# Sixty-four unused bytes between the on-chip pools of a two-layer decoder trunk

## The chip, the cores and the metric

The kernel runs on one core of one Trainium2 chip. The metric is device microseconds of one execution, the median of several runs.

## The reference

Two identical layers work on 512 tokens of width 1024 in float32. Each layer normalizes x, multiplies it by one combined input projection, runs four causal token mixers on parts of the result (forgetting attention, gated linear attention, retention, a state-space scan), gates and mixes them, projects back and adds to x. Then comes a SwiGLU block with 2816 hidden columns:

```python
for l in range(DEPTH):
    h = rms_norm(x, ln1[l])
    x = x + mixer_block(h, ...)        # u = h @ w_in; four mixers; gates; merged @ w_out
    h = rms_norm(x, ln2[l])
    x = x + swiglu(h, w_ffn_in[l], w_ffn_out[l])
```

Nearly all of the arithmetic is in the products with w_in, w_up_*, w_out, w_ffn_in and w_ffn_out.

## The kernel before

Activations are kept transposed: 128 channels on the partitions, 512 tokens along the free dimension, 4 bytes each. Every large product is made from matmuls of a stationary 128 x 128 block of weights and a moving block of 512 (or 256) columns. To keep float32 accuracy each operand is split in a high and a low part (`split`, L196: ScalarE copies to the rounded type, L197; VectorE subtracts, L198), and each product is three matmuls (`mm3`, L185, which calls `mm`, L183): high by high, high by low, low by high. Each matmul has a weight load of its own (128 columns), so matmuls and weight loads come in equal numbers, and the load for one matmul runs beside the matmul before it.

Weights stream in: SyncE's queue brings slabs of eight blocks (128 x 1024) to tiles `wr`, `convert` (L242) splits them to `wh` and `wl`. All three are in pool `wp`. The moving operands are:

- `xh`, `xl` (pool `bp`): the normalized x. They move in all products with w_in (512 columns) and in part of the products with w_ffn_in (256 columns).
- `t` (pool `tp`): results of the mixers and the merged sum. They move in the products with w_up_* and w_out (512 columns).
- `f` (pool `fp`): hidden activations. They move in the products with w_ffn_out (512 columns).
- `t1`, `t2`, `t3`, each with parts h and l (pool `tq`): sums of blocks of x. `strassen` (L1230) computes w_ffn_in by seven products (L1306) of 256 columns instead of eight; products 5, 6, 7 move t1, t2, t3, products 1 to 4 move quarters of xh and xl. In products 3, 5, 6, 7 the low part of the weights is a tile `l` from a pool of its own, `lp`; in products 1, 2, 4 it is `wl` from `wp`. The high part is always `wh`.

In two places the roles are turned: `wide` (L271) and `tokmajor` (L494) load xh and xl as the stationary operand, and the weights move (284 and 256 columns).

The pools are opened one behind the other and lie so in each partition. `cp`, `wp`, `bp`, `np`, `sp` live throughout; `phase` (L152) opens the pools of a mixer stage (gp, vp, bd, tp) or, at L1194, of a feed-forward stage (tq, ep, rp, lp, fp), which take each other's place. Sizes are multiples of 128 bytes except those of `cp` and `sp`. Where the tiles of a pool start, modulo 128 bytes, follows from the sizes of those before it:

| pool | holds | start modulo 128 |
|---|---|---|
| cp | x, constants | 0 (most) |
| wp | wr, wh, wl | 64 |
| bp, np | xh, xl; norm's sums | 64 |
| gp, vp, bd, tp | mixers: gates, v, states, t | 0 |
| tq, ep, rp, fp | t1 to t3; e; rq; f | 0 |
| lp | l | 0 |

Within a tile the operands of these matmuls begin at multiples of 512 bytes, so each has the remainder of its pool (the slices of `wide`, 1136 bytes apart, are the exception). The order of the instructions on each engine is set when the program is built, by the tile framework's scheduler; mixers and projections are interleaved by costs written in the code (`pull`, `drain`).

Of the kernel before, what the change touches and what calls it, by code (L numbers as in the profile page):

```python
# [10 lines left out]
F32 = mybir.dt.float32  # L11
# [7 lines left out]
P = 128  # L19
# [112 lines left out]
def trunk(ctx: ExitStack, tc: tile.TileContext, keys, qkeys, xin, pos, wst, wsq, par, ext, cst, out):  # L132
    nc = tc.nc
    V, A, G, T = nc.vector, nc.scalar, nc.gpsimd, nc.tensor

    cp = ctx.enter_context(tc.tile_pool(name="cp", bufs=1))
    wp = ctx.enter_context(tc.tile_pool(name="wp", bufs=3))
    bp = ctx.enter_context(tc.tile_pool(name="bp", bufs=1))
    np_ = ctx.enter_context(tc.tile_pool(name="np", bufs=4))
    sp = ctx.enter_context(tc.tile_pool(name="sp", bufs=3))  # L140
# [5 lines left out]
    def nm(s):  # L146
        uid[0] += 1
        return f"{s}{uid[0]}"

    pools = {}  # L150

    def phase(**bufs):  # L152
        st = ExitStack()
        for n, b in bufs.items():
            pools[n] = st.enter_context(tc.tile_pool(name=nm(n), bufs=b, reuse_waits="tile"))
        return st

    def mixers():
        return phase(gp=2, vp=2, bd=1, tp=33)
# [121 lines left out]
    scope = mixers()  # L281
# [139 lines left out]
    def layer(l, n1, scope):  # L421
# [769 lines left out]
        scope.close()  # L1191


        scope = phase(tq=1, ep=8, rp=5, lp=2, fp=9)  # L1194

        last = l == DEPTH - 1
        tb_ = {n: tuple(pools["tq"].tile([P, HK, H], F32R, tag=n + h, name=nm(n + h)) for h in "hl") for n in ("t1", "t2", "t3")}
# [232 lines left out]
    for l in range(DEPTH):  # L1430
        n1 = layer(l, n1, scope if l == 0 else mixers())
# [71 lines left out]
```

## Time and profile before

| | |
|---|---|
| median of 3 runs | 1750.88 us (1750.79 to 1751.33) |
| profiled execution | 1751.48 us, its span 1749.8 us |
| TensorE busy in the span | 1736.9 us (99%) |
| VectorE, ScalarE, GpSimd | 1215.5 (69%), 862.0 (49%), 225.9 us (13%) |
| HBM read | 191.27 MB, 111 GB/s over the span |

A matmul's duration in the trace covers its whole passage through the array, and matmuls overlap; what one of them costs is the distance from its start to the start of the next. This distance is called its gap below. In the timeline, rows of one kind that follow each other are merged (x2); starts are printed to 0.01 us, so a gap is read over many rows.

### The profile page before, as it was taken

Reading aid. Unit: us, or ns where it says so; the run is one execution under the profiler, and the core shown is the slowest. Engines: PE = TensorE matmul, PEld = TensorE weight load, DVE = VectorE, ACT = ScalarE, POOL = GpSimd, SP = SyncE. Lnnn points to the kernel's source line nnn. Section 1 sums busy time; section 2 is a strip of 40 time slices with the busy share of each in tenths; the row PEclk is TensorE's granted clock in tenths of the full one; section 3 lists DMA queues with packets and bytes.
Section 4 is the critical chain, followed back from the end, with each engine's and each line's share of the span. In section 5 each row is a group of like instructions: output and inputs, shape, how many; then the busy total and the mean of one; then the engine's idle time right before and its main releaser. Section 6 shows DMA issues by size and latency. Waiting matters only on the chain.

```text
span 1749.8 us, 25123 instructions
## 1 busy us (share of the span) xinstructions
PE 1736.9 (99%) x10140; PEld 1500.2 (86%) x10140; DVE 1215.5 (69%) x1683; ACT 862.0 (49%) x1190; POOL 225.9 (13%) x227
## 2 busy tenths in 40 slices
PE   9999999999999999999999999999999999999998
PEld 7878888888888999898988788888888898999987
DVE  5868576777667666675777666767776685666666
ACT  5425533555347455463544254335544473645543
POOL 2032120022101000000010311201220010100000
PEclk9999999999999999999999999999999999999999
DMA  6322222222236566575333222322222365656652
GB/s 202 97 83 62 86 72 85 84 85 85 84 97 171 157 140 172 130 183 108 86 102 114 68 67 73 96 73 84 85 84 85 119 169 146 147 156 140 173 107 99
DMA packets 54693, 195.00 MB, mean 111 GB/s; under 512 B 6064, under 2 KB 6448, under 8 KB 54576
## 3 DMA queue, kind: packets, MB, share of 16 engines
q1 hardware_dynamic: 45072, 160.45, 29.0%
q0 software_dynamic: 8640, 31.46, 10.4%
q8 instruction: 79, 1.29, 0.3%
q10 hardware_dynamic: 864, 1.48, 0.2%
q14 instruction: 38, 0.31, 0.1%
HBM read 191.27 MB, written 2.10 MB: 111 GB/s over the span
## 4 chain that ended last, share of the span: by engine, by line
PE 96%; DVE 2%; DMA 1%; ACT 1%; issue 0%; ACTq 0%; DVEq 0%
PE mm L183 64%; PE mx L183 31%; DVE wl L198 1%; PE mx L1058 0%; DMA x<-in_x_dram 0%; DMA t<-in_ext_dram 0%; ACT wh L197 0%; DVE f L1399 0%; DVE x L1400 0%; PE mx L658 0%; DVE t L352 0%; ACT L216 0%; ACT g L221 0%; DVE t L1147 0%; PE mx L930 0%
## 5 line engine op out<-in xcount | busy, mean ns | idle before, releaser
L197 ACT CAST wh<-wr 128x1024 fp32r<-128x1024 f32 (+1 forms) x240 | 249.8, 1042 | 394.5 <-PE mm L183 247.7
L183 PE MATMUL mm<-xh,wh 128*128 128x512 f32 (+1 forms) x1184 | 431.4, 364 | 0.8 <-DVE t L1147 0.8
L183 PE MATMUL mm<-xh,wl 128*128 128x512 f32 (+1 forms) x1184 | 430.5, 364 | 0.0
L183 PE MATMUL mm<-xl,wh 128*128 128x512 f32 (+1 forms) x1184 | 429.8, 363 | 0.0
L198 DVE TENSOR_TENSOR wl<-wr,wh 128x1024 fp32r<-128x1024 f32 (+1 forms) x220 | 282.0, 1283 | 117.9 <-ACT wh L197 109.7
L183 PEld LDWEIGHTS mm<-xh,wh 128*128 128x128 f32 x1184 | 223.5, 189 | 36.3 <-DVE t L1147 1.7
L183 PEld LDWEIGHTS mm<-xh,wl 128*128 128x128 f32 x1184 | 223.7, 189 | 34.8 <-issue 1.5
L183 PEld LDWEIGHTS mm<-xl,wh 128*128 128x128 f32 x1184 | 223.6, 189 | 33.7 <-issue 1.1
L183 PE MATMUL mm<-t,wh 128*128 128x512 f32 x448 | 142.5, 397 | 0.0
L183 PE MATMUL mx<-xl,wh 128*128 128x256 f32 (+1 forms) x448 | 140.4, 313 | 0.0
L183 PE MATMUL mx<-xh,wh 128*128 128x256 f32 (+1 forms) x448 | 137.8, 314 | 2.3 <-ACT wh L197 2.3
L1264 POOL DMA_DIRECT2D wl<-in_wsq_dram x60 | 51.9, 864 | 542.1 <-ACT wl L1263 322.9
L183 PE MATMUL mx<-f,wh 128*128 128x512 f32 x352 | 110.2, 395 | 0.0
L183 PE MATMUL mm<-f,wh 128*128 128x512 f32 x352 | 108.3, 396 | 0.0
L183 PEld LDWEIGHTS mm<-t,wh 128*128 128x128 f32 x448 | 83.2, 188 | 19.1
L198 DVE TENSOR_TENSOR l<-rq,wh 128x1024 fp32r<-128x1024 f32 x60 | 73.2, 1220 | 34.6 <-ACT wh L197 19.1
L183 PEld LDWEIGHTS mx<-xh,wh 128*128 128x128 f32 x448 | 84.6, 189 | 8.9 <-ACT wh L197 3.5
L183 PE MATMUL mx<-xh,wl 128*128 128x256 f32 (+1 forms) x288 | 91.9, 330 | 0.0
L183 PEld LDWEIGHTS mx<-xl,wh 128*128 128x128 f32 x448 | 84.7, 189 | 5.3
L183 PE MATMUL mm<-t,wl 128*128 128x512 f32 x224 | 88.5, 395 | 0.0
L183 PEld LDWEIGHTS mm<-f,wh 128*128 128x128 f32 x352 | 65.7, 188 | 16.2 <-ACT wh L197 1.0
L183 PEld LDWEIGHTS mx<-f,wh 128*128 128x128 f32 x352 | 65.4, 188 | 15.5
(275 smaller groups left out, 3470.8 us busy)
## 6 DMA issues: line engine op xcount, KB each, us to landing
wr<-in_wst_dram SPq DMA_DIRECT2D x216, 512.0 KB, 3.5
rq<-in_wsq_dram SPq DMA_DIRECT2D x60, 512.0 KB, 4.6
wl<-in_wsq_dram POOLq DMA_DIRECT2D x60, 512.0 KB, 5.7
wr<-in_wsq_dram SPq DMA_DIRECT2D x20, 512.0 KB, 5.0
out_dram<-x SPq DMA_DIRECT2D x8, 256.0 KB, 2.0
x<-in_x_dram SPq DMA_DIRECT2D x3, 512.0 KB, 6.9
wr<-in_wst_dram SPq DMA_DIRECT2D x4, 256.0 KB, 5.4
x<-in_x_dram SPq DMA_DIRECT2D x2, 256.0 KB, 4.5
```

The lines of the kernel that those rows point to most:

```text
L183: T.matmul(o, lhsT=l, rhs=r, start=start, stop=stop, skip_group_check=True)
L197: A.copy(out=hi, in_=src)
L198: V.tensor_tensor(out=lo, in0=src, in1=hi.bitcast(F32), op=ALU.subtract)
L1264: G.dma_start(out=lo, in_=wsq[j], accum_op=ALU.add)
```

## The change

No instruction is added or removed, and no wait. Pools of one tile of 64 bytes that nothing reads or writes are put between the pools:

```diff
     cp = ctx.enter_context(tc.tile_pool(name="cp", bufs=1))
+    gap = [ctx.enter_context(tc.tile_pool(name="gap0", bufs=1))]
     wp = ctx.enter_context(tc.tile_pool(name="wp", bufs=3))
+    gap.append(ctx.enter_context(tc.tile_pool(name="gap1", bufs=1)))
     bp = ctx.enter_context(tc.tile_pool(name="bp", bufs=1))
...
+    def pad(pool, n):
+        pool.tile([P, n // 4], F32, tag=nm("pad"), name=nm("pad"))
...
     def phase(**bufs):
+        if not pools:
+            for g in gap:
+                pad(g, 64)
         st = ExitStack()
+        pad(st.enter_context(tc.tile_pool(name=nm("gap"), bufs=1)), 64)
...
-        scope = phase(tq=1, ep=8, rp=5, lp=2, fp=9)
+        scope = phase(tq=1, ep=8, rp=5, g0=1, lp=2, g1=1, fp=9)
+        pad(pools["g0"], 64)
+        pad(pools["g1"], 64)
```

By the sums of the sizes, `wp` moves by 64 bytes, `bp`, `np` and `sp` by 128, the pools of a mixer stage and tq, ep, rp by 192, lp by 256, fp by 320. Modulo 128:

| pool | before | after |
|---|---|---|
| wp (wr, wh, wl) | 64 | 0 |
| bp, np (xh, xl) | 64 | 64 |
| gp, vp, bd, tp (t) | 0 | 64 |
| tq (t1 to t3), ep, rp | 0 | 64 |
| lp (l) | 0 | 0 |
| fp (f) | 0 | 64 |

So after the change the weights lie at 0 and the activations at 64 in every large product.

## Rows read from the trace of the kernel before

**Rows 1.** The page, parts 1 and 2: busy time and share of the engines (PEld is TensorE's weight load); the granted TensorE clock in 40 slices, in tenths.

```profile
PE 1736.9 (99%) x10140; PEld 1500.2 (86%) x10140; DVE 1215.5 (69%) x1683; ACT 862.0 (49%) x1190; POOL 225.9 (13%) x227
...
PEclk9999999999999999999999999999999999999999
```

**Rows 2.** TensorE's waits, whole span: engine, line, what it waited for: us in total, times, longest us. The two longest.

```profile
PE mm L183 <- DVE wl L198: 2.6, 6, 0.4
PE mx L183 <- ACT wh L197: 2.3, 3, 1.1
```

**Rows 3.** Busy time of each engine by stretch of the span (us, then busy us and instructions): the input projection with mixers, the products with w_out, the feed-forward of the first layer. The last three columns are the granted clock, the share of the DMA engines and GB/s.

```profile
178.00:466.00 288.00, 287.08 (x1549) 239.93 (x1548) 202.01 (x319) 136.72 (x192) 46.70 (x48) 1.00 0.26 81
478.00:530.00 52.00, 52.00 (x224) 41.75 (x223) 33.86 (x46) 24.23 (x32) 3.45 (x2) 1.00 0.33 105
...
555.00:875.00 320.00, 318.69 (x2177) 293.26 (x2177) 214.31 (x251) 170.62 (x229) 25.73 (x29) 1.00 0.58 142
```

**Rows 4.** Timeline of TensorE (start us, us, engine, line, operation, out<-in) in w_in's projection, weights and moving operand at 64: the first and the last of 15 matmuls in a row.

```profile
43.70 0.39 PE L183 MATMUL mm<-xh,wh 128*128 128x512 f32 x1
...
46.87 0.39 PE L183 MATMUL mm<-xh,wl 128*128 128x512 f32 x1
```

**Rows 5.** The same view in w_ffn_out, weights at 64, moving operand f at 0: from the first row's start to the last row's there are 12 matmuls.

```profile
600.42 0.63 PE L183 MATMUL mx<-f,wh 128*128 128x512 f32 x2
...
603.22 1.09 PE L183 MATMUL mx<-f,wh 128*128 128x512 f32 x4
```

**Rows 6.** The same view inside `strassen`, moving xh and xl at 64, 256 columns. First a product whose weights all lie at 64 (8 rows, the first and the last shown), then 12 matmuls of a product whose third matmul has its weights in l, at 0 (the first four and the one behind the twelfth).

```profile
568.42 0.28 PE L183 MATMUL mm<-xh,wl 128*128 128x256 f32 x1
...
569.26 0.28 PE L183 MATMUL mx<-xh,wh 128*128 128x256 f32 x1
569.38 0.28 PE L183 MATMUL mx<-xl,wh 128*128 128x256 f32 x1
569.50 0.28 PE L183 MATMUL mx<-xh,l 128*128 128x256 f32 x1
569.61 0.28 PE L183 MATMUL mx<-xh,wh 128*128 128x256 f32 x1
...
570.67 0.28 PE L183 MATMUL mm<-xh,wh 128*128 128x256 f32 x1
```

**Rows 7.** The same view where 512-column matmuls are followed by 256-column ones, all operands at 64.

```profile
553.62 0.39 PE L183 MATMUL mx<-xh,wl 128*128 128x512 f32 x1
553.85 0.28 PE L183 MATMUL mm<-xh,wh 128*128 128x256 f32 x1
553.96 0.28 PE L183 MATMUL mm<-xl,wh 128*128 128x256 f32 x1
554.08 0.28 PE L183 MATMUL mm<-xh,wl 128*128 128x256 f32 x1
554.20 0.28 PE L183 MATMUL mm<-xh,wh 128*128 128x256 f32 x1
```

**Rows 8.** The same view where one matmul with its weights at 0 (the constant cr, moving operand n at 64) stands in a row of 512-column matmuls with weights and moving operand at 64.

```profile
545.67 0.39 PE L183 MATMUL mx<-xl,wh 128*128 128x512 f32 x1
545.89 0.39 PE L183 MATMUL mx<-xh,wl 128*128 128x512 f32 x1
546.12 0.40 PE L183 MATMUL mm<-n,cr 128*128 128x512 f32 x1
546.35 0.39 PE L183 MATMUL mx<-xh,wh 128*128 128x512 f32 x1
...
547.27 0.39 PE L183 MATMUL mx<-xh,wh 128*128 128x512 f32 x1
```

**Rows 9.** Groups of matmuls by tile and shape over the whole span (xcount | busy us, mean ns of one | idle before): the first and the last of the eight groups that move t or f over 512 columns (1,920 matmuls), then of the six that move xh or xl over 512 (2,976), the seven that move xh or xl over 256 (1,920), the nine that move t1 to t3 over 256 (160 each, 1,440), and one of the three in which the weights move over 256 (128 each).

```profile
L183 PE MATMUL mm<-t,wh 128*128 128x512 f32 x448 | 142.5, 397 | 0.0
...
L183 PE MATMUL mx<-t,wl 128*128 128x512 f32 x64 | 25.2, 394 | 0.0
...
L183 PE MATMUL mm<-xh,wh 128*128 128x512 f32 x864 | 340.7, 394 | 0.8 <-DVE t L1147 0.8
...
L183 PE MATMUL mx<-xh,wl 128*128 128x512 f32 x128 | 46.7, 390 | 0.0
...
L183 PE MATMUL mm<-xh,wh 128*128 128x256 f32 x320 | 90.6, 283 | 0.0
...
L183 PE MATMUL mx<-xh,l 128*128 128x256 f32 x160 | 44.5, 278 | 0.0
...
L183 PE MATMUL mm<-t3l,wh 128*128 128x256 f32 x160 | 44.8, 281 | 0.0
...
L183 PE MATMUL mm<-t2h,l 128*128 128x256 f32 x160 | 42.1, 282 | 0.0
...
L183 PE MATMUL mm<-wh,xh 128*128 128x256 f32 x128 | 36.2, 283 | 0.0
```

**Rows 10.** Groups of VectorE's instructions by tile and shape, whole span: the subtraction of `split` with all its tiles at 64, and with rq and l at 0.

```profile
L198 DVE TENSOR_TENSOR wl<-wr,wh 128x1024 fp32r<-128x1024 f32 x216 | 278.4, 1290 | 117.6 <-ACT wh L197 109.7 <-PE mm L183 5.8 <-PE mx L183 1.2
L198 DVE TENSOR_TENSOR l<-rq,wh 128x1024 fp32r<-128x1024 f32 x60 | 73.2, 1220 | 34.6 <-ACT wh L197 19.1 <-PE mm L183 15.2
```

## The prediction

> **What bounds the kernel now.** I read the page first: TensorE is busy in 99% of the span, its clock is granted in full in every slice (the 2.4 GHz level), and no other engine passes 69% [rows 1]. Its waits for others come to a few us in all [rows 2]. So nothing in front of TensorE sets the time: the 10,140 matmuls do, one gap after the other. The stretches say the same of each stage: in the feed-forward VectorE works 214 of 320 us and the DMA engines 58% [rows 3], so there is room for a faster TensorE. Then I went to the timeline for the gap itself. At 2.4 GHz, 512 columns are 213.3 ns and 256 are 106.7. Nowhere is a gap that short:
>
> - xh, xl at 64 over weights at 64, 512 columns: 14 gaps in 3.17 us, 226.4 ns each [rows 4].
> - f at 0 over weights at 64, 512 columns: 12 gaps in 2.80 us, 233.3 ns [rows 5].
> - xh, xl at 64 over weights at 64, 256 columns: 7 gaps in 0.84 us, 120 ns [rows 6].
> - the same with every third matmul's weights in l, at 0: 12 gaps in 1.41 us, 117.5 ns, and the gap that is short in each three is that of the matmul over l, 0.11 us [rows 6].
>
> The excess is 13 to 20 ns per matmul, 10,140 times; it is all that an edit without instructions can win. 233.3 and 226.7, and 120 and 113.3, are 6.67 ns apart, 16 columns or 64 bytes of moving operand. So the excess seems to come in steps of 64 bytes. That is my reading of four rows, not something that a view prints.
>
> **The change, part by part.** It adds no instruction, DMA or wait, and no queue is passed; SyncE's and GpSimd's queues keep their order. All that moves is where a tile starts.
>
> *Moving t and f over 512 columns, 1,920 matmuls [rows 9].* They go from 0 to 64, their weights from 64 to 0. Rows 4 and 5 differ in the moving operand's half alone (the same tiles of weights, line and shape): 64 is better by 233.3 - 226.4 = 6.9 ns. In w_ffn_out (22 blocks x 8 columns x 3 x 2 layers = 1,056) and w_out (8 x 8 x 3 x 2 = 384) such matmuls follow each other without a break: 1,440 x 6.9 = 9.9 us. The 480 of w_up lie between mixer matmuls, and the means over the whole span (397 against 394 ns, breaks included [rows 9]) differ by less; I take half, 480 x 3.4 = 1.6 us. Together -11.5 us. Bounds: 0, and two steps instead of one (-25.6 us).
>
> *Moving xh, xl over 256 columns, 1,920 matmuls [rows 9].* The moving operand stays at 64, the weights go to 0. The trace has this case: the matmul over l lasts 278 ns on the average where the one over wh lasts 283 [rows 9]. One more row explains it. The first 256-column matmul behind a row of 512-column ones has a gap of 0.11 us too, the second 0.12 [rows 7]; its weights were loaded beside a longer matmul and long done. So I take 120 ns as 113 plus one step in which the weight load runs over into its own matmul, and weights at 0 as a load that doesn't. Then every such matmul gains 283 - 278 = 5 ns: (1,920 - 160) x 5 = -8.8 us. Bounds: 0 if only a switch between the halves helps, and 6.7 ns each (-11.8 us).
>
> *t1 to t3 over 256, 1,440 matmuls [rows 9].* From 0 over 64 (and 0 over l at 0; there the half of the weights makes no difference, 281 and 282) to 64 over 0: to 278 from 281.5, 3.5 x 1,440 = -5.0 us. Bounds: -6.7 x 1,440 = -9.6, and +1.5 x 1,440 = +2.2 if they end at the 283 of xh.
>
> *Moving xh, xl over 512 columns, 2,976 matmuls [rows 9].* The largest group and the open one: only the weights move, to 0. The nearest row is the constant cr. The matmul that runs while cr is loaded keeps 0.23 us [rows 8]; then from n over cr on, five gaps take 1.15 us, 230 ns, before the 227 is back. That shows a disturbance where the halves change, not a settled row. I take 0, since the gap beside the load didn't change; the bounds are a settled 230 (3.6 x 2,976 = +10.7 us) and one step less (-6.67 x 2,976 = -19.8 us).
>
> *The rest.* Where weights move and xh is stationary (384 of 256 columns, 192 of 284) the halves become those that t1 over wh has now: 283 to 281.5, -0.6 us. The some 1,300 small matmuls of the mixers get both operands at 64 instead of 0; their gaps are mostly waits and loads: 0, within 2 us. VectorE's subtraction took 1,290 ns with all at 64 and 1,220 with rq and l at 0 [rows 10]. Even 70 ns on each of some 300 are 21 us of an engine with a third of its time free; the cover is the weights' prefetch, and if it were gone TensorE's 2.6 us of waiting for wl [rows 2] would grow first.
>
> Sum: -11.5 - 8.8 - 5.0 + 0 - 0.6 = -25.9 us. The profiled execution took 1751.48 us, 0.6 above the median; 1751.48 - 25.9 = 1725.6, so 1725 for the median.
>
> **A rule that speaks against it.** Rows 4 and 5 show gaps that differ with a start address. The Trainium skill, page "TensorE: Matmul & The Clock Gate", section "Step-by-step: what each phase is for", says that TensorE has two independent read ports and that loading the next weights doesn't steal read bandwidth from the running matmul; by that, halves would be of no account and the change worth nothing. The page's section "Back-to-back issue gap" gives an isolated gap of N/2.4 + 2.5 ns, 215.8 at 512 columns as an estimate; the trace is 11 to 18 ns above it, so here the two reads do not look independent.
>
> **The rivals.**
>
> *Only the moving operand's half counts* (0.20). The gain of t and f stays, 256 columns remain at 120 and t1 to t3 rise by 2.2 us: 1750.9 - 11.5 + 2.2 = about 1742. For it: with t1 to t3 the weights' half makes no difference. Against it: l's 278.
>
> *A step less everywhere* (0.14). Weights at 0 free a step over 512 columns too: -19.8 us for xh and xl and some 9 more for t and f, 1725 - 29 = 1696. Against it: the gap beside the load of cr was as long as its neighbours.
>
> *Different halves are what costs* (0.10), the slower side. Rows 4 and 5 can also be read as same half (226.4) against different halves (233.3). After the change the halves differ everywhere: xh and xl over 512 pay 6.9 x 2,976 = +20.5 us, t and f gain nothing, the 256-column matmuls gain 1.5 ns each as t1 over wh has it (-2.6 us): 1768. It decides if the long rows of w_in settle at 233. Against it: xh over l is different halves and the shortest of all, and the gap before n over cr is not longer.
>
> *It does nothing that counts* (0.09): the remainder that matters is not that modulo 128 (f and t differ from xh in more address bits than one), or rows 4 and 5 differ for another reason, such as what surrounds them. 1751.
>
> **How the numbers follow.** The forecast (0.45) spans 1712 to 1738 by its own bounds. About 0.02 is left for the unforeseen. A measurement of this kernel can tell about 0.2%, 3.5 us. Faster: forecast, moving half, step less: 0.79, with a little of the rest 0.80; same 0.09; slower 0.11. The range takes in the forecast, the moving half and the step less, 1696 to 1748, 0.79 of the chance, and leaves the no-effect and the slower case out.
>
> **What would show it.** Right: timeline gaps of 226 to 228 ns in w_ffn_out; 0.11 us for all three matmuls of each three inside the Strassen products; groups that move xh over 256 at 278 ns; w_in's rows as before; TensorE's waits still a few us. If 256 columns stay at 120, the step on the weights' half failed. If w_in's gap is 220, that of the open group did; if it is 230 or more, the halves interact in a way that rows 8 only hinted at. Wrong as a whole: f still at 233, or TensorE waiting for VectorE because its writes became slower.

## Result and profile after

The changed kernel takes 1734.74 us (1734.62 to 1735.48) against 1751.11 us for the kernel before, measured beside it, a ratio of 0.9908 [0.9893, 0.9922]: 16.4 us less. The profiled execution took 1734.83 us, its span 1733.1 us. The prediction was 1725, with 1696 to 1748 as its range.

First what stayed the same. The page of the changed kernel, parts 1 and 2 (columns as in [rows 1]), then TensorE's two longest waits, as in [rows 2]. (`mm` is now L192, and `split` L206 and L207.)

```profile
PE 1720.2 (99%) x10140; PEld 1484.4 (86%) x10140; DVE 1212.9 (70%) x1683; ACT 862.7 (50%) x1190; POOL 228.1 (13%) x227
...
PEclk9999999999999999999999999999999999999999
```

```profile
PE mm L192 <- DVE wl L207: 2.7, 6, 0.4
PE mx L192 <- ACT wh L206: 2.4, 3, 1.1
```

The counts are those of before, the clock is granted in full throughout, the waits are 2.7 and 2.4 us against 2.6 and 2.3. TensorE still has nothing to wait for; all of the 16 us lies in the distances from start to start. By stretch (answers to [rows 3]):

```profile
178.00:466.00 288.00, 287.10 (x1550) 239.55 (x1548) 201.63 (x320) 137.54 (x194) 47.86 (x48) 1.00 0.27 82
478.00:530.00 52.00, 52.00 (x229) 42.73 (x228) 34.93 (x47) 24.14 (x32) 3.48 (x2) 1.00 0.33 105
555.00:875.00 320.00, 318.67 (x2214) 292.34 (x2213) 221.75 (x262) 176.07 (x236) 27.33 (x30) 1.00 0.59 145
```

The same time holds one matmul more in the input projection, five more with w_out and 37 more in the feed-forward. Now the gaps themselves. Timeline of the changed kernel, TensorE, in w_in (answers to [rows 4]; there are 14 gaps between the two rows) and in w_ffn_out (answers to [rows 5]; 15 gaps):

```profile
43.31 0.39 PE L192 MATMUL mm<-xh,wh 128*128 128x512 f32 x1
...
46.52 0.39 PE L192 MATMUL mm<-xh,wl 128*128 128x512 f32 x1
...
596.24 0.63 PE L192 MATMUL mx<-f,wh 128*128 128x512 f32 x2
...
599.74 0.63 PE L192 MATMUL mx<-f,wh 128*128 128x512 f32 x2
```

w_in: 3.21 us / 14 = 229.3 ns, up from 226.4. w_ffn_out: 3.50 / 15 = 233.3 ns, not moved at all, although both of its operands were. The same view in the Strassen products (answers to [rows 6]): 16 gaps over weights in wh and wl, then 12 with every third matmul's weights in l:

```profile
567.08 0.28 PE L192 MATMUL mm<-xh,wl 128*128 128x256 f32 x1
...
568.89 0.28 PE L192 MATMUL mx<-xh,wh 128*128 128x256 f32 x1
...
570.25 0.28 PE L192 MATMUL mm<-xh,wh 128*128 128x256 f32 x1
```

1.81 / 16 = 113.1 ns and 1.36 / 12 = 113.3 ns, against 120 and 117.5. The groups by shape (answers to [rows 9], mean ns of one next to last):

```profile
L192 PE MATMUL mm<-xh,wh 128*128 128x512 f32 x864 | 342.2, 396 | 0.8 <-DVE t L1156 0.8
L192 PE MATMUL mm<-t,wh 128*128 128x512 f32 x448 | 141.5, 395 | 0.0
L192 PE MATMUL mx<-f,wh 128*128 128x512 f32 x352 | 110.3, 396 | 0.0
...
L192 PE MATMUL mm<-xh,wh 128*128 128x256 f32 x320 | 88.6, 277 | 0.0
...
L192 PE MATMUL mx<-xh,l 128*128 128x256 f32 x160 | 44.2, 276 | 0.0
...
L192 PE MATMUL mm<-t3l,wh 128*128 128x256 f32 x160 | 44.0, 276 | 0.0
...
L192 PE MATMUL mm<-wh,xh 128*128 128x256 f32 x128 | 35.6, 278 | 0.0
```

Over 256 columns every group that moves xh, xl or t1 to t3 is now at 276 to 278 ns, where they were at 278 to 283 [rows 9]; over 512, xh went up from 394 to 396 and t down from 397 to 395. Durations mix breaks and settled rows, so I also took the start of every matmul from each trace, put it beside the program's order, and summed the gaps by the tile that moves. These sums (us, with the mean gap in ns, breaks left out) carry the rest of this text; the last five columns are kernels of the experiments:

| moves, columns (matmuls) | before | after | f128 | w_only | l128 | a_only | zero512 |
|---|---|---|---|---|---|---|---|
| xh, xl, 512 (2,976) | 689.6 (228.0) | 694.5 (229.7) | 694.4 | 695.2 | 694.4 | 688.7 (227.7) | 689.0 (227.8) |
| f, 512 (1,056) | 250.8 (233.4) | 250.4 (233.2) | 246.2 (229.1) | 244.5 (227.5) | 246.2 | 244.6 (227.3) | 245.0 (227.3) |
| t, 512 (864) | 202.5 | 199.3 | 199.3 | 198.4 | 199.3 | 197.3 | 197.3 |
| xh, xl, 256 (1,920) | 228.9 (119.2) | 219.2 (114.1) | 219.0 | 226.1 (117.7) | 223.5 (116.3) | 230.3 (119.9) | 218.1 (113.5) |
| t1 to t3, 256 (1,440) | 170.0 (118.0) | 163.9 (113.8) | 164.0 | 172.8 (120.0) | 167.6 (116.4) | 173.0 (120.1) | 163.8 (113.6) |
| wh, wl, 256 and 284 (576) | 71.9 | 69.9 | 69.9 | 70.6 | 69.9 | 71.9 | 71.9 |
| all TensorE | 1743.5 | 1726.9 | 1722.3 | 1737.6 | 1730.6 | 1735.9 | 1715.2 |

After less before: -9.7 for xh and xl over 256, -6.1 for t1 to t3, -3.2 for t, -2.0 for moving weights, -0.4 for f, and +4.9 for xh and xl over 512; -16.6 for all of TensorE.

### The profile page after: what moved, and what is told of

It is laid out like the page before. It is cut to its first block, busy times and chain, and to the rows that moved or that the text cites. A ratio compares the mean times of both kernels' runs of the same rounds, so it can differ in the third digit from the quotient of the medians.

```text
span 1733.1 us, 25123 instructions
## 1 busy us (share of the span) xinstructions
PE 1720.2 (99%) x10140; PEld 1484.4 (86%) x10140; DVE 1212.9 (70%) x1683; ACT 862.7 (50%) x1190; POOL 228.1 (13%) x227
## 4 chain that ended last, share of the span: by engine, by line
PE 96%; DVE 2%; DMA 1%; ACT 1%; issue 0%; ACTq 0%
PE mm L192 64%; PE mx L192 31%; DVE wl L207 1%; PE mx L1067 0%; DMA x<-in_x_dram 0%; DMA t<-in_ext_dram 0%; ACT wh L206 0%; DVE f L1410 0%; DVE x L1411 0%; PE mx L667 0%; DVE t L361 0%; ACT L225 0%; ACT g L230 0%; DVE t L1156 0%; PE mx L859 0%
## 5 line engine op out<-in xcount | busy, mean ns | idle before, releaser
L206 ACT CAST wh<-wr 128x1024 fp32r<-128x1024 f32 (+1 forms) x240 | 249.9, 1043 | 395.6 <-PE mm L192 246.0
L192 PE MATMUL mm<-xh,wh 128*128 128x512 f32 (+1 forms) x1184 | 430.8, 364 | 0.8 <-DVE t L1156 0.8
L192 PE MATMUL mm<-xh,wl 128*128 128x512 f32 (+1 forms) x1184 | 430.4, 364 | 0.0
L192 PE MATMUL mm<-xl,wh 128*128 128x512 f32 (+1 forms) x1184 | 429.3, 363 | 0.0
L207 DVE TENSOR_TENSOR wl<-wr,wh 128x1024 fp32r<-128x1024 f32 (+1 forms) x220 | 279.8, 1273 | 121.0 <-ACT wh L206 112.6
L192 PEld LDWEIGHTS mm<-xh,wh 128*128 128x128 f32 x1184 | 222.8, 188 | 37.1 <-DVE t L1156 1.7
L192 PEld LDWEIGHTS mm<-xh,wl 128*128 128x128 f32 x1184 | 222.8, 188 | 35.7 <-issue 1.5
L192 PEld LDWEIGHTS mm<-xl,wh 128*128 128x128 f32 x1184 | 222.8, 188 | 34.8 <-issue 1.1
L192 PE MATMUL mm<-t,wh 128*128 128x512 f32 x448 | 141.5, 395 | 0.0
L192 PE MATMUL mx<-xl,wh 128*128 128x256 f32 (+1 forms) x448 | 138.9, 310 | 0.0
L192 PE MATMUL mx<-xh,wh 128*128 128x256 f32 (+1 forms) x448 | 136.2, 311 | 2.4 <-ACT wh L206 2.4
L192 PE MATMUL mx<-f,wh 128*128 128x512 f32 x352 | 110.3, 396 | 0.0
L192 PE MATMUL mm<-f,wh 128*128 128x512 f32 x352 | 108.2, 396 | 0.0
L192 PEld LDWEIGHTS mm<-t,wh 128*128 128x128 f32 x448 | 83.4, 188 | 17.8
L207 DVE TENSOR_TENSOR l<-rq,wh 128x1024 fp32r<-128x1024 f32 x60 | 73.2, 1220 | 32.9 <-ACT wh L206 18.5
L192 PEld LDWEIGHTS mx<-xh,wh 128*128 128x128 f32 x448 | 84.1, 188 | 9.4 <-ACT wh L206 3.6
L192 PE MATMUL mx<-xh,wl 128*128 128x256 f32 (+1 forms) x288 | 91.2, 328 | 0.0
L192 PEld LDWEIGHTS mx<-xl,wh 128*128 128x128 f32 x448 | 84.2, 188 | 5.2
L192 PE MATMUL mm<-t,wl 128*128 128x512 f32 x224 | 87.7, 392 | 0.0
L192 PEld LDWEIGHTS mm<-f,wh 128*128 128x128 f32 x352 | 65.9, 188 | 15.7 <-ACT wh L206 0.6
L192 PEld LDWEIGHTS mx<-f,wh 128*128 128x128 f32 x352 | 65.7, 188 | 15.0
```

What stands on the lines that cost most here:

```text
L192: T.matmul(o, lhsT=l, rhs=r, start=start, stop=stop, skip_group_check=True)
L206: A.copy(out=hi, in_=src)
L207: V.tensor_tensor(out=lo, in0=src, in1=hi.bitcast(F32), op=ALU.subtract)
```

## Experiments

The tiles' starts were read from the memory layout of each program. Modulo 128, as the change is described, f and t look alike. Modulo 256 they don't:

| kernel | wh, wl | xh, xl | t, t1 to t3 | f | l |
|---|---|---|---|---|---|
| before | 192 | 192 | 128 | 128 | 128 |
| after | 0 | 64 | 64 | 192 | 128 |
| f128 | 0 | 64 | 64 | 64 | 128 |
| w_only | 0 | 64 | 0 | 0 | 0 |
| l128 | 0 | 64 | 64 | 64 | 0 |
| a_only | 192 | 192 | 192 | 192 | 192 |
| zero512 | 64; in Strassen 0 and 128 | 64 | 64 | 64 | 128 |

The theory under test: what counts is the difference d, the moving operand's start less the weights' start, modulo 256. Before, xh has d = 0 and t and f have 192; after, xh and t have 64, and f has 192 again.

**1. Starts by themselves (probe).** A small kernel with rows of 48 matmuls on constant tiles: moving tiles ma to md (and on to mh) and weights sa to sd, each 64 bytes further than the one before it; then ma over sa once more with one of the two 16, 32 or 48 bytes further in.

```diff
+    for cols in (512, 256):
+        for s in "abcd":
+            for m in "abcd":
+                row("", s, m, cols)
+        for m in "efgh":
+            row("", "a", m, cols)
+        for o in (4, 8, 12):
+            row("", "a", "a", cols, mo=o)
+            row("", "a", "a", cols, so=o)
```

> Only matmuls, none of the decoder: rows of 48 matmuls of 128 x 128 weights over 512 and then 256 columns, float32r, nothing else running. The weights' tile starts at 0, 64, 128 or 192 bytes modulo 512 (sa to sd), the moving tile at 0 to 448 (ma to mh), all pairs of the first four, and starts 16, 32 and 48 bytes off. Difference theory: the settled gap depends on the moving operand's start minus the weights', modulo 256: 227 ns at 0, 229 at 64, 233 at 192 over 512 columns (120, 113, 118 over 256), so ma over sa = mb over sb = mc over sc, and mb over sa = mc over sb. Half theory (that of the forecast): over 512 columns the moving operand's remainder modulo 128 decides alone, 227 for mb and md, 233 for ma and mc whatever the weights; over 256 the weights' remainder, 113 for sa and sc, 120 for sb and sd. No difference between 128 and 0, or 192 and 64, in that theory.

It took 456.31 us. Timeline, rows of 48 matmuls (start us, duration of the row), 512 columns and then 256:

```profile
55.63 11.36 PE L54 MATMUL p<-ma,sb 128*128 128x512 f32 x48
66.83 11.06 PE L54 MATMUL p<-mb,sb 128*128 128x512 f32 x48
77.73 11.17 PE L54 MATMUL p<-mc,sb 128*128 128x512 f32 x48
88.74 11.32 PE L54 MATMUL p<-md,sb 128*128 128x512 f32 x48
99.90 11.31 PE L54 MATMUL p<-ma,sc 128*128 128x512 f32 x48
...
144.19 11.16 PE L54 MATMUL p<-ma,sd 128*128 128x512 f32 x48
155.19 11.32 PE L54 MATMUL p<-mb,sd 128*128 128x512 f32 x48
...
322.30 5.82 PE L54 MATMUL p<-ma,sb 128*128 128x256 f32 x48
327.96 5.91 PE L54 MATMUL p<-mb,sb 128*128 128x256 f32 x48
333.71 5.82 PE L54 MATMUL p<-mc,sb 128*128 128x256 f32 x48
...
379.15 5.61 PE L54 MATMUL p<-mc,sd 128*128 128x256 f32 x48
384.60 5.90 PE L54 MATMUL p<-md,sd 128*128 128x256 f32 x48
```

The distance to the next row's start over 48 gives the gap: ma over sb (d = 192) 11.20 us, 233.3 ns; mb over sb (0) 10.90, 227.1; mc over sb (64) 11.01, 229.4; md over sb (128) 11.16, 232.5; ma over sd (64 once more) 11.00. Over 256 columns ma over sb has 5.66 us, 117.9 ns, and mb over sb 5.75, 119.8. In the second half of each row, where the gaps have settled, they are, for all four starts of the weights, and again for moving starts 256 bytes further:

| d | 512 columns | 256 columns |
|---|---|---|
| 0 | 226.7 ns | 120.0 ns |
| 64 | 228.8 | 117.8 |
| 128 | 232.2 | 118.7 |
| 192 | 233.3 | 117.8; in two of five rows 113.3 |

ma over sb and ma over sd have the same halves of 128 bytes in both operands and differ by 4.5 ns (233.3 against 228.8 settled). No reading by halves survives that; the difference does. Over 256 columns one of its figures missed: it had 113 ns at 64, where 117.8 came. The last entry is odd: the same d gave 117.8 over sb and 113.3 for mc over sd (5.45 us for the 48).

Between the multiples of 64 the gap doesn't run evenly. By the starts in the trace (the timeline merges these rows of ma over sa), 512 columns take 231.9, 233.3 and 233.4 ns with the moving operand 16, 32 and 48 bytes further in, and 226.7, 233.3 and 233.3 with the weights so. Each was tried at one pair of tiles, so whether the difference alone decides there too isn't shown; all that follows has starts at multiples of 64.

**2. f brought to 64 (f128).** If f didn't gain because its d stayed at 192, 128 bytes more in front of its pool must make it 64.

```diff
-        pad(pools["g1"], 64)
+        pad(pools["g1"], 192)
```

> The changed kernel with f alone moved by another 128 bytes: its remainder modulo 128 stays 64, its start minus the weights' goes from 192 to 64 modulo 256. Difference theory: the gaps of w_ffn_out go from 233.3 to the 228.9 that w_out has now, 1,056 x 4.4 = 4.6 us less than the changed kernel, about 1730, ratio to before 0.988. Half theory: nothing changes, 1734.7, ratio 0.991; then w_ffn_out is slow for a reason of its place.

1730.35 us, ratio 0.9882 [0.9869, 0.9896]. Timeline in w_ffn_out, 15 gaps:

```profile
596.10 0.62 PE L192 MATMUL mx<-f,wh 128*128 128x512 f32 x2
...
599.53 0.62 PE L192 MATMUL mx<-f,wh 128*128 128x512 f32 x2
```

3.43 / 15 = 228.7 ns where the change left 233.3, and f's sum falls by 4.2 us, nearly all of the 4.4 us between the two kernels. Modulo 128 f stands where it stood: the halves of 128 bytes are refuted inside the kernel too.

**3. Only the weights' gaps (w_only).** No unused tile at the head of a phase or inside the feed-forward stage.

```diff
     def phase(**bufs):
...
-        pad(st.enter_context(tc.tile_pool(name=nm("gap"), bufs=1)), 64)
...
-        scope = phase(tq=1, ep=8, rp=5, g0=1, lp=2, g1=1, fp=9)
-        pad(pools["g0"], 64)
-        pad(pools["g1"], 64)
+        scope = phase(tq=1, ep=8, rp=5, lp=2, fp=9)
```

> The two gaps around the weights alone, none between the stage pools: weights at 0, xh and xl at 64, t, t1 to t3, l and f at 0 modulo 256. Difference theory: t and f over 512 columns settle at 226.7 like xh before (difference 0), t1 to t3 at 120; against before -5.5 us for t, -7.0 for f, +3.0 for t1 to t3, and as in the changed kernel +4.9 for xh over 512, -9.7 for xh over 256, -1.9 where the weights move: 1734.9, as fast as the whole change. Half theory: t and f stay at 233.3, t1 to t3 at 118; only the xh terms come: 1744.

1745.49 us, ratio 0.9969 [0.9957, 0.9981]. The total is near what the halves gave, but its gaps are not theirs: f at 227.5 ns and t1 to t3 at 120.0 are what the difference says (d = 0). It falls short of the difference's 1734.9 by 10.6 us, and the largest part, 6.9 us (226.1 against 219.2), is xh and xl over 256 columns: they were expected at 114 ns as in the changed kernel and stay at 117.7. Over wh and wl their d is 64 in both kernels; only over l it differs (192 there, 64 here). The rest is spread over the other terms. So the gap of one matmul is not a function of its own d.

**4. Rows of threes (triples).** The decoder's pattern, high by high, low by high, high by low, alone: 64 combinations of the three differences, in 48 matmuls each.

```diff
+            for n_, (w, m) in enumerate(((wh[c], mh), (wh[c], ml[b]), (wl[d], mh))):
+                T.matmul(ps[:, :cols], lhsT=w[:, sl], rhs=m[:, :cols], start=i == 0 and n_ == 0,
+                         stop=i == TRIPLES - 1 and n_ == 2, skip_group_check=True)
```

> Only matmuls again, in the decoder's threes (high weights over the high moving part, high over low, low weights over high), 16 threes a row, 512 and then 256 columns. mh starts at 0, the low moving part (la to ld), the high weights (ha to hd) and the low weights (wa to wd) at 0, 64, 128 or 192 modulo 256: 64 patterns of three differences (moving minus weights). If a row's gap is the mean of its three single gaps, 512 columns lie between 226.7 (all 0) and 233.3, and nothing is below 226.7; 256 columns between 117 and 120. If a mixed pattern tips a row into another state, as I now think of the changed kernel's 256-column rows (differences 64, 64 and, over l, 192: 113.3 instead of the 117.8 that the first probe has for 64 alone), the row with la, hd, wb (64, 64, 192) is at 113.3 over 256 columns, and some mixed rows over 512 lie a step below 226.7, at 220.

It took 1093.79 us. Timeline, 256 columns: differences (64, 64, 192), 18 gaps, and (64, 64, 64), 23 gaps.

```profile
1003.29 0.28 PE L58 MATMUL p<-mh,hd 128*128 128x256 f32 x1
...
1005.33 0.28 PE L58 MATMUL p<-mh,hd 128*128 128x256 f32 x1
...
1013.73 0.28 PE L58 MATMUL p<-mh,hd 128*128 128x256 f32 x1
...
1016.44 0.28 PE L58 MATMUL p<-mh,wd 128*128 128x256 f32 x1
```

2.04 / 18 = 113.3 and 2.71 / 23 = 117.8 ns. Of the 64 patterns only (64, 64, 192) and (192, 192, 64) settle at 113.3. The patterns of the kernel before come out too: (0, 0, 0) at 120.0, (0, 0, 64) at 117.9, (192, 192, 0) at 117.8, beside 120, 117.5 [rows 6] and the 118.0 of t1 to t3. Over 512 columns (0, 0, 0) is the shortest of all 64, 226.7, and the longest is 235.6; nothing is at 220, which I had thought possible. Mixed patterns are not the means of their parts.

**5. l at the difference of the rest (l128).** f128, and in front of l as well 128 bytes more, so that every matmul over 256 columns has d = 64.

```diff
-        pad(pools["g0"], 64)
+        pad(pools["g0"], 192)
```

> As the kernel with f moved by 128, and the tile l moved by another 128 bytes: its remainder modulo 128 stays 0, the moving operand's start minus that of l goes from 192 to 64 modulo 256, as it is over wh. Two-state theory: 64 everywhere keeps rows of 256 columns in the slow state of the first probe (117.8), nothing tips them: +7 us for xh, +5.6 for t1 to t3, about 1743. Theory of the forecast (weights at 0 modulo 128 don't run over into their matmul): no change, 1730.

1738.62 us, ratio 0.9931 [0.9917, 0.9945]. Timeline of one execution: 17 gaps in the first layer, then 18 gaps at the head of a later stretch.

```profile
567.34 0.28 PE L192 MATMUL mm<-xl,wh 128*128 128x256 f32 x1
...
569.34 0.28 PE L192 MATMUL mx<-xh,wh 128*128 128x256 f32 x1
...
814.76 0.28 PE L192 MATMUL mx<-xh,wh 128*128 128x256 f32 x1
...
816.80 0.28 PE L192 MATMUL mx<-xh,wh 128*128 128x256 f32 x1
```

2.00 / 17 = 117.6 and 2.04 / 18 = 113.3 ns: the same tiles, the same d, two levels. The program has eight long stretches of Strassen products (312 to 480 matmuls). In this execution five ran at 117.8 from end to end and three at 113.3 from end to end. In the changed kernel, whose l has d = 192, seven of eight begin at 117.8 and all are at 113.3 once their first product over l has run. Timeline of the changed kernel, 23 gaps before and 23 behind that product:

```profile
627.76 0.28 PE L192 MATMUL mx<-xh,wh 128*128 128x256 f32 x1
...
630.46 0.28 PE L192 MATMUL mx<-xh,wl 128*128 128x256 f32 x1
...
633.37 0.28 PE L192 MATMUL mx<-t1h,wh 128*128 128x256 f32 x1
...
635.98 0.28 PE L192 MATMUL mx<-t1h,l 128*128 128x256 f32 x1
```

2.70 / 23 = 117.4, then 2.61 / 23 = 113.5 ns. The three stretches at 113.3 are worth 4.9 us by their gap sums; without them l128 would stand at 1743.5, where the first of its two forecasts has it. So a pattern of 64 alone keeps the level that it starts with, and a 192 among them brings it to the lower one. What decides the level at the start of a stretch, these runs don't show. That l128's five times spread over 5 us (1737.0 to 1742.06) where f128's lie within 0.2 us fits a choice made anew in each execution, but only one execution of it was traced.

**6. Only the phase's gap (a_only).** The opposite of 3: weights, xh and xl where they were, t, t1 to t3, f and l moved up to the same 192.

```diff
-    gap = [ctx.enter_context(tc.tile_pool(name="gap0", bufs=1))]
...
-    gap.append(ctx.enter_context(tc.tile_pool(name="gap1", bufs=1)))
...
     def phase(**bufs):
         if not pools:
-            for g in gap:
-                pad(g, 64)
+            pass
...
-        scope = phase(tq=1, ep=8, rp=5, g0=1, lp=2, g1=1, fp=9)
-        pad(pools["g0"], 64)
-        pad(pools["g1"], 64)
+        scope = phase(tq=1, ep=8, rp=5, lp=2, fp=9)
```

> The change with the three unused tiles around the weights left out (gap0, gap1) and those inside the FFN stage left out (g0, g1); only the one unused tile of 64 bytes at the head of each phase stays. Weights, xh and xl keep the starts of before (192 modulo 256), and t, f, t1 to t3 and l go from 128 to 192. Theory of the difference: moving t and f against weights is now difference 0, so f takes 244.5 us in place of 250.8 (-6.3) and t 198.4 in place of 202.5 (-4.1); xh and xl over 512 columns stay at 689.6; over 256 columns every row of three has differences 0, 0, 0, so 120.0 ns for xh and xl (+1.5) and for t1 to t3 (+2.9). Sum -6.0: 1745.1 us, ratio 0.9966. Theory of different halves of 128 bytes (the one that the change was described with): moving operands and weights now share the upper half everywhere, so t and f, which were in the other half's start at 0 modulo 128, lose what they had: 1750 us or more, ratio 1.000 to 1.003.

1743.9 us, ratio 0.9958 [0.9946, 0.9971]: the difference's 1745.1 within 1.2 us, and out of reach for the theory of different halves. Timeline: 18 gaps in w_ffn_out, and 15 in a Strassen product that is at 120 before the change as well.

```profile
568.08 0.28 PE L189 MATMUL mm<-xh,wh 128*128 128x256 f32 x1
...
569.88 0.28 PE L189 MATMUL mx<-xh,wh 128*128 128x256 f32 x1
...
595.83 0.62 PE L189 MATMUL mx<-f,wh 128*128 128x512 f32 x2
...
599.91 0.62 PE L189 MATMUL mx<-f,wh 128*128 128x512 f32 x2
```

4.08 / 18 = 226.7 ns for f, 1.80 / 15 = 120.0 over 256 columns. With every operand at the same start, each width has one gap: of the four in the probe's table the shortest at 512 columns and the longest at 256. The two widths want opposite things.

**7. Each width its own starts (zero512).** From f128, weights tiles 256 bytes longer; `convert` uses them from byte 64 on (d = 0 over 512 columns), the Strassen stage from 0 for wh and from 128 for wl (64, 64, 192 always).

```diff
+    def WT(tag, at):
+        return wp.tile([P, SLAB * P + 64], F32R, tag=tag, name=nm(tag))[:, at:at + SLAB * P]
...
-            hi = wp.tile([P, SLAB * P], F32R, tag="wh", name=nm("wh"))
-            lo = wp.tile([P, SLAB * P], F32R, tag="wl", name=nm("wl"))
+            hi = WT("wh", 16)
+            lo = WT("wl", 16)
...
-                lo = wp.tile([P, SLAB * P], F32R, tag="wl", name=nm("wl"))
+                lo = WT("wl", 32)
...
-                hi = wp.tile([P, SLAB * P], F32R, tag="wh", name=nm("wh"))
+                hi = WT("wh", 0)
```

> The kernel of the run f128 with the weights tiles wh and wl made 256 bytes longer, so that their starts can be chosen inside the tile: for the 512-column stages both start at 64 modulo 256, as the moving operands xh, xl, t and f do there (difference 0); for the 256-column products wh starts at 0 and wl at 128, so that every row of three has the differences 64, 64, 192 whether its low half is wl or l. Nothing else is changed. Theory of the difference: every settled gap over 512 columns is the one of difference 0, 226.7 ns, also over xh and xl: against f128, xh and xl over 512 go from 694.4 us back to the 689.6 us that they had before the change (-4.8), f from 246.2 to the 244.5 us that it had at difference 0 in w_only (-1.7), merged t of w_out some -0.8; over 256 columns the rows stay in the 113.3 ns state from the start of each stretch (219.0 us to some 217.7, -1.3); the weights-moving products go to difference 0 and back to some 120 ns (+1.0). Sum -7.6: 1722.7 us, ratio to the kernel before 0.984. Theory that only the start of the tile's allocation or the moving half counts: no gain over 512 columns against f128, so 1730 us, ratio 0.988. A result above 1727 us speaks against the difference as the whole cause.

1723.1 us, ratio 0.9838 [0.9825, 0.9852], the shortest of all and 0.4 us from what the table of gaps gave. Timeline in w_in (15 gaps), a Strassen product (15) and w_ffn_out (12):

```profile
43.11 0.39 PE L192 MATMUL mm<-xh,wh 128*128 128x512 f32 x1
...
46.51 0.39 PE L192 MATMUL mm<-xh,wh 128*128 128x512 f32 x1
...
567.22 0.28 PE L192 MATMUL mm<-xh,wh 128*128 128x256 f32 x1
...
568.92 0.28 PE L192 MATMUL mx<-xh,wh 128*128 128x256 f32 x1
...
595.80 0.62 PE L192 MATMUL mx<-f,wh 128*128 128x512 f32 x2
...
598.52 1.07 PE L192 MATMUL mx<-f,wh 128*128 128x512 f32 x4
```

226.7, 113.3 and 226.7 ns. All eight Strassen stretches are at 113.3 from their first matmuls on.

## Why the prediction was right, and where it was not

The frame held: TensorE alone sets the time, nothing else became late, and the sum had to be made from gaps. The sign and most of the size came from the 256-column matmuls, and that the total came out within the range is in part luck: -15.8 of the -16.5 us are terms whose size was good and whose mechanism was not, while t and f fell 7.9 us short and xh, xl over 512 lost 4.9. Of the prediction's own signs, 0.11 us for all three matmuls of a Strassen three and waits of a few us came; f still at 233, its sign of being wrong as a whole, came too, and w_in's rows didn't stay as before. The terms:

| term | predicted | measured |
|---|---|---|
| f over 512 | -7.3 | -0.4 |
| t over 512 | -4.2 | -3.2 |
| xh, xl over 256 | -8.8 | -9.7 |
| t1 to t3 | -5.0 | -6.1 |
| xh, xl over 512 | 0 | +4.9 |
| moving weights | -0.6 | -2.0 |
| sum | -25.9 | -16.5 |

- **Moving t and f** (-11.5) is the step that failed: it measured -3.6. It took [rows 4, 5] as two values of one variable, the moving operand's half of 128 bytes. They differ in the difference of the two starts: 0 against 192. The change turned t's into 64, which is worth 4.5 ns (233.3 to 228.9 in w_out) and not 6.9, and left f's at 192, because f's pool moved by 320 bytes and the weights by 64, 256 apart. The table of starts modulo 128 hid this. f128 gives f 4.2 us, and in a_only and zero512, at d = 0, f has the whole 6.7 ns (233.3 to 226.7).
- **xh and xl over 512** (0, bounds -19.8 and +10.7) ended inside its bounds, on the side of a loss: d went from 0, the best, to 64. The probe has 228.8 ns for it against 226.7, and w_in's gap is now 229.3. The 230 ns behind n over cr [rows 8], which gave the bound, lie near that by chance: they were a passing disturbance, as the prediction read them. Of those five matmuls only the first, n at 192 over cr at 128 modulo 256, has d = 64; the four behind it have 0. In zero512, where n over cr has d = 192 and the four behind it 0, the same five gaps take 1.15 us again (the two rows under this list). The term became +4.9 us and not +10.7 because over all 2,976 the mean of before was already 228.0, not 226.4, and that of after is 229.7.
- **xh and xl over 256, and t1 to t3** (-13.8) measured -15.8. The number was good and the mechanism was not. "One step in which the weight load runs over into its own matmul", ended by weights at 0, would have made every row of w_only and l128 short; in w_only xh and xl stayed at 117.7 and t1 to t3 at 120.0, in l128 five of eight stretches at 117.8. What the change did was to bring l to d = 192 beside a 64 of the rest, and with that the rows are at 113.3. With weights moved alone, t1 to t3 became 2.0 ns longer than before.
- **Moving weights**: d became 192 where it was 0, so 121.6 went to 116.7 ns in place of the 1.5 ns taken from t1.
- **VectorE** kept the 1,220 ns of its subtraction into l and went from 1,290 to 1,279 into wl, so its cover was not needed.

Timeline of zero512, n over cr and the matmul five gaps later:

```profile
543.31 0.40 PE L192 MATMUL mm<-n,cr 128*128 128x512 f32 x1
...
544.46 0.39 PE L192 MATMUL mx<-xh,wh 128*128 128x512 f32 x1
```

Of the rivals, "only the moving half counts" and "different halves cost" fall by the probe's ma over sb and ma over sd, alike in halves and not in gaps, and by f128. "A step less everywhere" falls by w_in: it had 220 there, and 229.3 came. "It does nothing that counts" had one thing right in its reason, that the remainder modulo 128 is not the one that matters; it was only not zero.

In the probe the gap goes from 227.1 to 233.3 ns when nothing but the moving operand's start changes against weights that stay. The Trainium skill, page "TensorE: Matmul & The Clock Gate", section "Step-by-step: what each phase is for", says that loading the next weights doesn't take read bandwidth from the running matmul. For these operands the measurement differs: the gap depends on both addresses at once, so the two reads don't look independent. That it is the reads that meet, and where, is not shown by any run here.

## What to carry to other kernels

Where TensorE is at 99% and each matmul has its own weight load, read the gap to a hundredth of its length and compare it between tiles; a start address is worth up to 3% of a 512-column gap and 6% of a 256-column one. Compute the difference of both operands' starts modulo 256 for each kind of product before moving a pool, and expect that one padding helps some and harms others: offsets inside the tiles, chosen by stage, gave 1.6% where the gaps between pools gave 0.9%, or 1.2% with f's start put right (f128). All of this is from one type, float32 in its rounded form. A rule drawn from rows that differ in two things (here half and difference) should be tried on rows that differ in one.

## What was not expected of the hardware

- The gap depends on the moving operand's start less the weights' start modulo 256: 226.7, 228.8, 232.2 and 233.3 ns over 512 columns at differences of 0, 64, 128 and 192. It doesn't run evenly in between: the moving operand only 16 bytes further in gives 231.9 (probe).
- Over 256 columns the order is another, 120.0, 117.8, 118.7 and 117.8 ns, and a second level of 113.3 ns exists: at difference 64 a stretch of 312 to 480 matmuls stays at 117.8 or at 113.3 throughout (l128).
- 113.3 ns is 6.6 ns above the 106.7 that 256 periods of 2.4 GHz make, and 226.7 is 13.4 above the 213.3 of 512. No settled row among the 64 patterns came closer.
